# Second layer's experts: half of the tokens gather their experts' rows, the other half multiplies in float32

## The chip, the cores and the metric

The kernel runs on one core of a Trainium2 chip. The metric is the device time of one execution in microseconds, as the median of several runs. A profile of one further execution shows what each engine did in it: PE (TensorE), DVE (VectorE), ACT (ScalarE), POOL (GpSimd) and the queues of transfers, SP's above all.

## What is computed

The program is two blocks of two layers each over 256 tokens of 1024 numbers. The change lies in the first block, in the experts of its second layer. They see the latent tokens alone, two blocks of 128:

```python
def block(hb):                      # 128 tokens at a time
    n = hb.shape[0]
    q = (hb @ w_q).reshape(n, PEER_HEADS, 2, PEER_DK_HALF)      # 8 heads
    s = jnp.einsum('nhpk,pek->nhpe', q, keys)                   # 128 keys for each half
    v_top, i_top = lax.top_k(s, PEER_TOPK)                      # 16
    cand = (v_top[:, :, 0, :, None] + v_top[:, :, 1, None, :]).reshape(n, PEER_HEADS, PEER_TOPK * PEER_TOPK)
    sc, pos = lax.top_k(cand, PEER_TOPK)
    i1 = jnp.take_along_axis(i_top[:, :, 0], pos // PEER_TOPK, axis=-1)
    i2 = jnp.take_along_axis(i_top[:, :, 1], pos % PEER_TOPK, axis=-1)
    e = i1 * N_KEYS + i2                                        # one of 16384 experts
    g = jax.nn.softmax(sc.astype(jnp.float32), axis=-1).astype(hb.dtype)
    a = jax.nn.gelu(jnp.einsum('nhkd,nd->nhk', u_tab[e], hb)) * g
    return jnp.einsum('nhk,nhkd->nd', a, v_tab[e])
```

Each token has 8 x 16 = 128 chosen experts, and an expert is one row of u_tab and one row of v_tab. `x + mod[5] * _peer(h)` is the layer's result.

## The kernel before

A Tile program: the engines' instructions are recorded by helpers and put in order by a scheduler, so an engine's order is not quite that of the code.

There are two ways to the experts' sum. The **dense** way multiplies all tokens with all 16384 rows of U, in 128 blocks of 128 experts (`first`), passes the products through gelu into the tile A, multiplies A by the tokens' weights, zero for experts that were not chosen (`peer_weights`, which builds the weights of 8 tokens at a time from comparisons, f16 products on PE into ps_G and a product on DVE), and multiplies A with the 128 blocks of V (`second`). The **gathered** way fetches for each of the 128 choices the rows of U of 128 tokens by one indirect transfer of POOL (`rows_of`), multiplies them with the tokens on DVE, which sums along the row (line 1409), and later fetches for each token its 128 rows of V and sums them on PE (ps_gv), 32 tokens to a tile.

In the first layer (`peer0`, line 1453) the context tokens go the gathered way beside the dense way of the latent tokens; its first product is float32 (`lin_32`), its second has three parts. In the second layer (`peer`, line 1268, called from line 2323) all 256 latent tokens go the dense way, and both products have three parts: a weight tile is loaded into one of four `raw` buffers by SP's queue, ACT casts it to fp32r (line 350, whi), and DVE or every few times POOL subtracts (line 353, wlo); `hilo` does the same to the activations. `mm3` then makes three matmuls of one. A is a ring of 77 blocks, so the second product starts before the first ends, and a block of U is followed by one of V.

`peer_front` makes the choice: the norm, 16 tiles of queries and their scores, the 16 best of each, the 256 sums of a head, the 16 best of them, and the experts' numbers by comparisons, all on DVE. It yields between its steps, and the caller puts U blocks there. Of `mem_norm`, which prepares the memory tokens for the next block, steps stand in the loops as `side`. The norm of the memory tokens uses the same raw buffers.

Of the kernel before, what the change touches and what calls it, by code (L numbers as in the profile page):

```python
# [188 lines left out]
def prep(I):  # L189
# [18 lines left out]
    for l in range(2):  # L208
# [22 lines left out]
        if l == 0:  # L231
            A["Ur"] = I["peer_u"][l]
# [65 lines left out]
class Kern:  # L298
# [296 lines left out]
    def ctx_ahead(self):  # L595

        while not self.ctx_done:
# [479 lines left out]

    RANGES = {1: (36, 46, 46), 2: (36, 46, 46)}
    RING = {1: 77, 2: 66}
# [4 lines left out]
    def peer_open(self, es, ngroups, ranges=None):  # L1084
# [7 lines left out]
        self.nh = min(ngroups, 2)  # L1092
        self.RG = max(ranges or self.RANGES[ngroups])
# [6 lines left out]
    def peer_front(self, l, s, st, rows=False):  # L1100
# [19 lines left out]
        for j in range(16):  # L1120
            ps = self.psb("ps_q")
            if l == 0:
# [14 lines left out]
        if rows:  # L1137
            self.token_major(h, st)
        else:
            st.update({n: pe.tile([P, NT], FH, tag=n, bufs=self.nh, name=n) for n in ("i1T", "i2T")})  # L1140
            gT = st["gT"] = pe.tile([P, NT // self.TB, 2, self.TB], FH, tag="gT", bufs=self.nh, name="gT")
        for b in range(2):
# [37 lines left out]
            if rows:  # L1180
# [37 lines left out]
    def peer_weights(self, st, A, s0, i0, n):  # L1218
# [5 lines left out]
        def use(t0, pss):  # L1224
            for half in range(NH):
                pv = pss[half][:, :HB * n].rearrange("p (t i) -> p i t", t=HB)
                th = slice(t0 + half * HB, t0 + half * HB + HB)
# [10 lines left out]
        for t0 in range(0, NT, TB):  # L1238
# [13 lines left out]
            if t0:  # L1252
                use(t0 - TB, pss)
# [14 lines left out]
    def peer(self, l, streams, side=()):  # L1268

        nc = self.nc  # L1270
        es = ExitStack()
        self.ctx_done = False
        self.peer_open(es, len(streams))
        pe = self.pe
        self.keys = pe.tile([P, 2, P], FT, name="keys")
        nc.sync.dma_start(self.keys, self.A[f"keys{l}"].rearrange("p (q e) -> p q e", q=2))
        if l:
            self.gains(l, 1)
        sts = [{} for _ in streams]
        fronts = [self.peer_front(l, s, st) for s, st in zip(streams, sts)]  # L1280
        R = self.RING[len(streams)]
        total = P * len(streams)
        A = pe.tile([P, R, NT], FT, name="A")
        pos = {"u": 0, "v": 0}

        def first():
            c = pos["u"]
            pos["u"] += 1
            w = self.weight(self.A[f"U{l}"][c % P])
            ps = self.psb("ps_U")  # L1290
            self.lin_t(w, sts[c // P]["h"], 0, NT, ps)
            nc.scalar.activation(A[:, c % R], ps[:, :NT], AF.Gelu_apprx_tanh)

        acc = None

        def second(c):
            t = A[:, c % R]
            a = (pe.tile([P, NT], FR, tag="a_hi", bufs=2, name="a_hi"),
                 pe.tile([P, NT], FR, tag="a_lo", bufs=2, name="a_lo"))
            self.hilo(a[0], a[1], t)  # L1300
            w = self.weight(self.A[f"V{l}"][c % P])
            for b in range(2):
                bs = slice(b * P, (b + 1) * P)
                for n in range(2):
                    ns = slice(n * 512, (n + 1) * 512)
                    self.mm3(acc[2 * b + n], (a[0][:, bs], a[1][:, bs]), (w[0][:, ns], w[1][:, ns]),
                             c % P == 0, c % P == P - 1)

        def ahead():
            return pos["u"] < total and pos["u"] < pos["v"] + R and sts[pos["u"] // P].get("h") is not None  # L1310


        self.pool_each = 2
        for k, _ in enumerate(fronts[0]):
            self.pool_each = 1 if k in PE1 else 2
            for _ in range(k % 2 if k <= 32 else 2):
                if ahead():
                    first()
        side = fronts[1:] + [f(pe) for f in side]
        ranges = []  # L1320
        for g in range(len(streams)):
            i0 = 0
            for n in self.RANGES[len(streams)]:
                ranges.append((g * P + i0, g, i0, n))
                i0 += n
        gens = [self.peer_weights(sts[g], A, c0 % R, i0, n) for c0, g, i0, n in ranges]
        NB = NT // self.TB + 1
        more = R - pos["u"]
        for k, _ in enumerate(gens[0]):
            for _ in range((k + 1) * more // NB - k * more // NB):  # L1330
                first()
        self.pool_each = 4
        nr, left = 1, NB
        for c in range(total):
            pos["v"] = c
            if c % P == 0:
                acc = [self.psa("ps_acc") for _ in range(4)]
            if nr < len(ranges):
                c0, g, i0, n = ranges[nr]
                if pos["u"] >= c0 + n:  # L1340
                    if left == NB and g and i0 == 0:
                        while "done" not in sts[g]:
                            self.advance(side)
                    k = -(-left // max(1, c0 - c - 1))
                    self.pool_each = 1 if pos["u"] == total else 4
                    for _ in range(min(k, left)):
                        next(gens[nr])
                        left -= 1
                    if left == 0:
                        nr, left = nr + 1, NB  # L1350
            second(c)
            self.pool_each = 4
            pos["v"] = c + 1
            if ahead():
                first()
            self.advance(side)
            if c % P == P - 1:
                self.peer_out(l, streams[c // P], acc)
                self.ctx_done = True
        self.advance(side, 1000)  # L1360
        es.close()

# [3 lines left out]
    def gather_open(self, st):  # L1366

        nc, pe = self.nc, self.pe
        st["ht"] = pe.tile([P, 2, D], FT, name="ht")
        st["g"] = pe.tile([P, 2, P], FT, name="gr")  # L1370
        st["d"] = pe.tile([P, 2, P], FT, name="dots")
        st["e"] = pe.tile([P, 2, P], U32, name="er")
        st["eT"] = pe.tile([P, 2, P], U32, name="eT")
# [6 lines left out]
    def token_major(self, h, st):  # L1380

        nc = self.nc
        for b in range(2):
# [973 lines left out]
```

## Time and profile before

| | us |
|---|---|
| median of 3 runs | 4083.49 |
| lowest, highest | 4080.9, 4084.05 |
| the profiled execution | 4071.07 |
| its span in the trace | 4069.2 |

The trace is one execution, and its stretches are told in us from the span's start. An engine's busy time is the union of its instructions; PEld is the loading of stationary operands, which runs beside PE. A matmul's recorded duration includes time in which the next is already under way, so prices of products are taken from the spacing of their starts. A float32 matmul of the code appears as two instructions. The granted clock is given as a share of 2.4 GHz.

### The profile page before, as it was taken

The page shows a single profiled execution, that of the slowest core. Times are in us where ns is not written, and L with a number is a line of the kernel's source. Part 1 is how long each engine was busy: PE and PEld are TensorE (multiplying, and loading weights), DVE is VectorE, ACT ScalarE, POOL GpSimd, SP SyncE. Part 2 cuts the span into 40 slices and gives each one's busy share as a digit, 9 for nine tenths or more (in the row PEclk, how much of TensorE's full clock was granted, in tenths as well). Part 3 has the DMA queues.
Part 4 walks back from the last instruction along what each step waited for, and adds up shares of the span by engine and source line. Part 5 has one row for each costly group of instructions (what it writes and reads, how often), then busy time and mean ns, then how long its engine had stood idle before and what let it go on. Part 6 is the DMA issues. An engine that isn't in the chain of part 4 may idle for free. (4 is left out here: it accounts for less than half of the span.)

```text
span 4069.2 us, 69007 instructions
## 1 busy us (share of the span) xinstructions
PE 3736.2 (92%) x26811; PEld 3164.7 (78%) x26811; DVE 2718.9 (67%) x5739; ACT 1522.1 (37%) x2552; POOL 1333.6 (33%) x916
## 2 busy tenths in 40 slices
PE   8999996866898889999799988999999999999999
PEld 6777875755676666666589988889778899999999
DVE  5833368788787642374585799886785666864785
ACT  6433320111121211233455443444334646553554
POOL 0022205432435434455314456322442131231122
PEclk9999997987898999999899999999999999999999
DMA  5254238965989889999545544556446413565355
GB/s 211 70 166 140 79 119 281 334 218 192 355 306 365 333 312 354 336 353 403 194 130 163 160 146 126 160 168 191 150 146 189 144 48 113 178 198 179 92 178 151
DMA packets 228952, 827.48 MB, mean 203 GB/s; under 512 B 25736, under 2 KB 27408, under 8 KB 228624
## 3 DMA queue, kind: packets, MB, share of 16 engines
q1 hardware_dynamic: 154752, 554.08, 42.2%
q0 software_dynamic: 73728, 268.47, 17.8%
q8 instruction: 211, 3.46, 0.3%
q14 instruction: 117, 0.96, 0.1%
q10 hardware_dynamic: 144, 0.52, 0.0%
HBM read 821.91 MB, written 1.06 MB: 202 GB/s over the span
## 5 line engine op out<-in xcount | busy, mean ns | idle before, releaser
L350 ACT CAST whi<-raw 128x1024 fp32r<-128x1024 f32 (+1 forms) x774 | 802.0, 1039 | 975.8 <-DMA raw<-in_V 322.0
L353 POOL TENSOR_TENSOR wlo<-raw,whi 128x1024 fp32r<-128x1024 f32 (+1 forms) x230 | 570.6, 2482 | 1457.8 <-ACT whi L350 1308.5
L353 DVE TENSOR_TENSOR wlo<-raw,whi 128x1024 fp32r<-128x1024 f32 (+1 forms) x544 | 670.2, 1233 | 459.8 <-ACT whi L350 454.6
L1394 POOL DMA_INDIRECT gb<-in_Ur,er x256 | 329.6, 1288 | 536.0 <-DVE gb L1409 300.3
L323 PE MATMUL ps_U<-h,raw 128*128 128x256 f32 x2048 | 483.1, 392 | 23.9 <-ACT A L1481 23.7
L323 PEld LDWEIGHTS ps_U<-h,raw 128*128 128x128 f32 x2048 | 398.5, 197 | 93.7 <-ACT A L1481 24.6
L323 PE MATMUL ps_acc<-wlo,a_hi 128*128 128x512 f32 x1024 | 420.6, 411 | 46.2 <-DVE wlo L353 43.7
L323 PE MATMUL ps_acc<-whi,a_hi 128*128 128x512 f32 x1024 | 430.2, 424 | 15.4 <-ACT whi L350 15.4
L323 PE MATMUL ps_acc<-whi,a_lo 128*128 128x512 f32 x1024 | 415.7, 406 | 0.0
L1409 DVE SCALAR_TENSOR_TENSOR gb<-gb,ht 128x1024 f32<-128x1024 f32 x256 | 310.2, 1223 | 124.3 <-DMA gb<-in_Ur,er 123.1
L363 ACT CAST a_hi<-A 128x256 fp32r<-128x256 f32 x256 | 103.5, 405 | 568.4 <-PE ps_acc L323 525.5
L323 PE MATMUL ps_U<-h_hi,whi 128*128 128x256 f32 x1024 | 294.3, 287 | 7.9 <-DVE A L1232 5.4
L323 PE MATMUL ps_U<-h_hi,wlo 128*128 128x256 f32 x1024 | 291.4, 285 | 8.4 <-DVE wlo L353 6.5
L323 PE MATMUL ps_U<-h_lo,whi 128*128 128x256 f32 x1024 | 290.8, 284 | 0.0
L323 PEld LDWEIGHTS ps_acc<-wlo,a_hi 128*128 128x128 f32 x1024 | 200.5, 196 | 95.3 <-DVE wlo L353 53.3
L323 PE MATMUL ps_in<-hh_hi,whi 128*128 128x256 f32 (+1 forms) x776 | 265.9, 345 | 1.7 <-ACT hh_hi L568 1.7
L323 PE MATMUL ps_in<-hh_hi,wlo 128*128 128x256 f32 (+1 forms) x776 | 262.3, 339 | 1.1 <-POOL wlo L353 1.1
L323 PEld LDWEIGHTS ps_acc<-whi,a_hi 128*128 128x128 f32 x1024 | 198.6, 195 | 83.0 <-ACT whi L350 20.7
L323 PE MATMUL ps_in<-hh_lo,whi 128*128 128x256 f32 (+1 forms) x776 | 262.9, 340 | 0.0
L364 DVE TENSOR_TENSOR a_lo<-A,a_hi 128x256 fp32r<-128x256 f32 x256 | 117.5, 460 | 201.8 <-ACT a_hi L363 199.7
L1394 POOL DMA_INDIRECT gb<-in_V,eT x170 | 182.5, 1073 | 178.0 <-PE ps_gv L323 145.4
L323 PEld LDWEIGHTS ps_acc<-whi,a_lo 128*128 128x128 f32 x1024 | 200.6, 196 | 47.6 <-DVE a_lo L364 0.6
(636 smaller groups left out, 8748.9 us busy)
## 6 DMA issues: line engine op xcount, KB each, us to landing
raw<-in_U SPq DMA_DIRECT2D x256, 512.0 KB, 4.3
raw<-in_V SPq DMA_DIRECT2D x256, 512.0 KB, 4.5
raw<-in_win SPq DMA_DIRECT2D x96, 512.0 KB, 3.8
raw<-in_wup SPq DMA_DIRECT2D x88, 512.0 KB, 3.8
raw<-in_wada SPq DMA_DIRECT2D x80, 512.0 KB, 4.8
raw<-in_wq SPq DMA_DIRECT2D x48, 512.0 KB, 4.5
raw<-in_gwin SPq DMA_DIRECT2D x37, 512.0 KB, 3.7
raw<-in_wdn SPq DMA_DIRECT2D x32, 512.0 KB, 4.1
```

The costliest lines, as they stand in the source:

```text
L323: self.nc.tensor.matmul(o, l, r, start=start, stop=stop)
L350: nc.scalar.copy(hi[:, :f], raw[:, :f])
L353: eng.tensor_sub(lo[:, :f], raw[:, :f], hi[:, :f].bitcast(FT))
L363: (copy or self.nc.scalar.copy)(hi, src)
L364: self.nc.vector.tensor_sub(lo, src, hi.bitcast(FT))
L1394: self.nc.gpsimd.indirect_dma_start(t, None, table, bass.IndirectOffsetOnAxis(ap=at, axis=0), bounds_check=P * P - 1, oob_is_err=False)
L1409: nc.vector.scalar_tensor_tensor(t, t, 1.0, st["ht"][:, b], op0=OP.mult, op1=OP.mult, accum_out=st["d"][:, b, j:j + 1])
```

## The change

The host passes U as plain rows for the second layer too (`Ur1`). `peer` with its ring is replaced by `peer1`. The tokens of block 0 go the gathered way, those of block 1 the dense way, in float32 without splits: 8 matmuls of 128 columns to a block of U and 2 of 512 columns to a block of V. A holds all 128 blocks for 128 tokens. The choice is still made for all 256 tokens, now in float32, and ends for block 0 with the experts' numbers (er), their transpose (eT) and the weights (gr) as in the first layer, for block 1 as before. The rows land in six buffers that held the split weights, and after the U rows in the tile of the tokens as a seventh. `peer_weights` gets a first token T0 and works in two ranges of 64 blocks.

```diff
     def peer_front(self, l, s, st, rows=()):
...
-        if l == 0:
-            h = self.hs[s]
-        else:
-            h = tuple(pe.tile([P, KC, NT], FR, name=n) for n in ("h_hi", "h_lo"))
+        h = self.hs[s]
...
-            if l == 0:
-                self.lin_32(self.load_w(self.A["wq0"][j]), h, ps[:, :NT])
-            else:
-                self.lin_t(self.weight(self.A[f"wq{l}"][j]), h, 0, NT, ps)
+            self.lin_32(self.load_w(self.A[f"wq{l}"][j]), h, ps[:, :NT])
...
         if rows:
-            self.token_major(h, st)
-        else:
+            self.token_major(h, st, rows)
+        if len(rows) < 2:
...
-    def gathered(self, st):
+    def gathered(self, st, l, s, nb):
...
-        U, V = self.A["Ur"], self.A["V0"].rearrange("a b d -> (a b) d")
+        U, V = self.A[f"Ur{l}"], self.A[f"V{l}"].rearrange("a b d -> (a b) d")
...
+    RANGES1 = (64, 64)
+
+    def peer1(self, side=()):
...
+        self.gather_open(st, 1)
+
+        st["buf"] += [self.sp.tile([P, D], FT, tag=t, bufs=3, name="gb") for _ in range(3) for t in ("whi", "wlo")]
+        self.hs = (None, pe.tile([P, KC, NT], FT, name="h32"))
+        A = pe.tile([P, P, P], FT, name="A")
...
+        gath = self.gathered(st, 1, 1, 1)
+
+        def units(n):
+            credit[0] += n
+            while credit[0] >= 1 and not self.gathered_all:
+                next(gath)
+                credit[0] -= 1
+
+        def first():
+            c = u[0]
+            u[0] += 1
+            ps = self.psb("ps_U")[:, :P]
+            self.lin_32(self.load_w(self.A["U1"][c]), st["h"][:, :, P:], ps)
+            nc.scalar.activation(A[:, c], ps, AF.Gelu_apprx_tanh)
+
+        for k, _ in enumerate(self.peer_front(1, 1, st, (0,))):
+            first()
+            if "blocks" in st:
+                units(1)
+        side = [f(pe) for f in side]
+        gens = [self.peer_weights(st, A, i0, i0, 64, P) for i0 in (0, 64)]
+        while u[0] < P:
+            first()
+            units(1.5)
+            self.advance(side)
+            if u[0] >= 64:
+                next(gens[0], None)
...
+        acc = [self.psa("ps_acc") for _ in range(2)]
+        for c in range(P):
+            if c >= 4 and c % 3 == 0 or c == 63:
+                for _ in range(1 if c < 63 else P):
+                    next(gens[1], None)
+            w = self.load_w(self.A["V1"][c])
+            for n in range(2):
+                self.mm(acc[n], A[:, c], w[:, n * 512:(n + 1) * 512], c == 0, c == P - 1)
+            units(1.05)
+            self.advance(side)
...
-        self.peer(1, (1,), [lambda pool: self.mem_norm(0, 20)])
+        self.peer1([lambda pool: self.mem_norm(0, 20)])
```

The scheduler turns this into new orders. In the order's rows h_19920 is the normed tokens, raw a weight tile, gb a row buffer, Z_19910 and Z_19911 the tiles that take the gathered tokens' weights, dots the sums of the row products, R and sq the sums of squares of the memory tokens; a line's number is that of the kernel it is from.

**PE, at the end of the front.** Before, the last products of a query tile and the first of a U block:

```order
L323 MATMUL ps_q<-h_hi,whi 128x256
L323 MATMUL ps_q<-h_lo,whi 128x256
L323 MATMUL ps_q<-h_hi,wlo 128x256
L323 MATMUL ps_U<-h_hi,whi 128x256
L323 MATMUL ps_U<-h_lo,whi 128x256
L323 MATMUL ps_U<-h_hi,wlo 128x256
```

Now, from the last scores to the transposes of the experts' numbers (ps_eT for block 0, ps_iT for block 1):

```order
L322 MATMUL ps_U<-h_19920,raw 128x128 x8
L322 MATMUL ps_q<-h_19920,raw 128x256 x8
L322 MATMUL ps_U<-h_19920,raw 128x128 x8
L322 MATMUL ps_s<-keys,qT 128x128 x2
L322 MATMUL ps_U<-h_19920,raw 128x128 x8
L327 MATMUL ps_ht<-cst,h_19920 128x128 x8
L322 MATMUL ps_U<-h_19920,raw 128x128 x48
L327 MATMUL ps_eT<-cst,idx 128x128
L322 MATMUL ps_U<-h_19920,raw 128x128 x56
L327 MATMUL ps_iT<-cst,idx 128x128
```

The three kinds of part products are gone; 33 blocks of U stand ahead of ps_ht and six behind it, ahead of the transpose that the gathered tokens' choice ends with.

**POOL, through the stage.** Before, the low parts of weights (wlo) and the sums of squares of `mem_norm`:

```order
L353 TENSOR_TENSOR wlo<-raw,whi 128x1024
L527 TENSOR_TENSOR R<-R,sq 128x256 x2
L353 TENSOR_TENSOR wlo<-raw,whi 128x1024 x80
L527 TENSOR_TENSOR R<-R,sq 128x256 x7
L353 TENSOR_TENSOR wlo<-raw,whi 128x1024 x59
```

Now, from the clearing of the two Z tiles:

```order
L1271 MEMSET Z_19910 128x512
L1271 MEMSET Z_19911 128x512
L1289 DMA gb<-in_Ur,er 128x1024 x44
L526 TENSOR_TENSOR R<-R,sq 128x256
L1289 DMA gb<-in_Ur,er 128x1024
L526 TENSOR_TENSOR R<-R,sq 128x256 x6
L1289 DMA gb<-in_Ur,er 128x1024 x83
L1289 DMA gb<-in_V,eT 128x1024 x4
```

All 128 gathers of U stand in POOL's order, with the seven sums among them, and those of V follow directly.

**PE, at the turn to the second product.** Before, where a block of V is followed by one of U:

```order
L323 MATMUL ps_acc<-whi,a_lo 128x512
L323 MATMUL ps_acc<-whi,a_hi 128x512
L323 MATMUL ps_acc<-wlo,a_hi 128x512
L323 MATMUL ps_acc<-whi,a_lo 128x512
L323 MATMUL ps_U<-h_hi,whi 128x256
L323 MATMUL ps_U<-h_lo,whi 128x256
L323 MATMUL ps_U<-h_hi,wlo 128x256
```

Now:

```order
L322 MATMUL ps_U<-h_19920,raw 128x128 x390
L322 MATMUL ps_acc<-raw,A 128x512 x24
L327 MATMUL ps_aT<-cst,dots 128x128
L322 MATMUL ps_acc<-raw,A 128x512
L322 MATMUL ps_gv<-gb,Z_19910 32x256 x8
```

U and V no longer alternate: 390 matmuls, the last 48 blocks of U and a part of one, stand in a row, then twelve blocks of V, then the transpose of the row products (ps_aT), and only behind it the first rows of V.

## Rows read from the trace of the kernel before

**Rows 1.** page's first part: busy us (share of span) and instructions

```profile
PE 3736.2 (92%) x26811; PEld 3164.7 (78%) x26811; DVE 2718.9 (67%) x5739; ACT 1522.1 (37%) x2552; POOL 1333.6 (33%) x916
```

**Rows 2.** stretches: length, busy PE PEld DVE ACT POOL (x), PEclk, DMA, GB/s

```profile
2239.00:2346.00 107.00, 102.14 (x843) 100.87 (x842) 83.15 (x327) 52.36 (x90) 42.26 (x17) 0.98 0.53 161
2346.00:2450.00 104.00, 81.10 (x634) 79.61 (x633) 101.70 (x184) 42.11 (x67) 54.82 (x22) 0.92 0.45 142
2450.00:2890.00 440.00, 430.92 (x3672) 392.03 (x3672) 340.07 (x499) 193.01 (x295) 154.44 (x65) 0.99 0.55 165
2890.00:3157.00 267.00, 250.52 (x1498) 195.45 (x1497) 195.68 (x273) 109.97 (x163) 101.33 (x42) 0.99 0.53 158
```

**Rows 3.** groups, same stage: form xcount | busy us, mean ns | idle before

```profile
L323 PE MATMUL ps_U<-h_hi,whi 128*128 128x256 f32 x1024 | 294.3, 287 | 7.9 <-DVE A L1232 5.4 <-ACT whi L350 2.6
L323 PE MATMUL ps_acc<-whi,a_hi 128*128 128x512 f32 x512 | 208.8, 408 | 0.0
L350 ACT CAST whi<-raw 128x1024 fp32r<-128x1024 f32 x273 | 285.7, 1048 | 254.8 <-PE ps_U L323 90.0 <-POOL wlo L353 73.3 <-issue 65.2
L353 POOL TENSOR_TENSOR wlo<-raw,whi 128x1024 fp32r<-128x1024 f32 x137 | 347.9, 2541 | 547.9 <-ACT whi L350 543.3 <-DMA raw<-in_U 3.7 <-POOL wlo L353 0.6
L353 DVE TENSOR_TENSOR wlo<-raw,whi 128x1024 fp32r<-128x1024 f32 x136 | 168.2, 1238 | 60.8 <-ACT whi L350 60.3
```

**Rows 4.** TensorE's timeline, first layer: start us, us, engine, line, form

```profile
1016.63 3.61 PE L323 MATMUL ps_U<-h,raw 128*128 128x256 f32 x16
1020.08 0.38 PE L328 MATMUL ps_adaT<-cst,adar 128*128 128x128 f32 x2
```

**Rows 5.** one tile's products: ns min/median/max, first and last start us

```profile
L323 PE MATMUL ps_c<-bl,raw x128: 273/275/377, 3733.4 to 3749.6; 128*128 128x128 f32 x128
```

**Rows 6.** TensorE's timeline around two gathered rows of the first layer

```profile
1841.36 0.39 PE L323 MATMUL ps_acc<-whi,a_lo 128*128 128x512 f32 x1
1841.67 1.07 PE L323 MATMUL ps_gv<-gb,Z 128*32 128x256 f32 x16
1842.68 0.50 PE L323 MATMUL ps_acc<-whi,a_hi 128*128 128x512 f32 x1
```

**Rows 7.** the weight products' group in the stage of rows 3

```profile
L323 PE MATMUL ps_G<-Pg,P 128*128 128x46 f16 x1024 | 40.7, 185 | 16.5 <-DVE Pg L1250 14.7 <-ACT a_hi L363 0.2
```

**Rows 8.** stretches of the first layer's experts, columns as in rows 2

```profile
1000.00:1380.00 380.00, 322.36 (x1907) 248.12 (x1907) 286.33 (x590) 74.11 (x132) 181.28 (x139) 0.90 0.94 348
1040.00:1060.00 20.00, 16.54 (x59) 12.75 (x60) 13.29 (x22) 3.08 (x5) 10.56 (x8) 0.73 1.00 378
1360.00:1380.00 20.00, 12.84 (x53) 8.81 (x51) 12.10 (x21) 3.17 (x5) 9.94 (x9) 0.74 0.95 363
1560.00:1640.00 80.00, 80.00 (x579) 55.46 (x578) 18.28 (x35) 14.94 (x27) 40.66 (x38) 1.00 0.97 358
1800.00:1940.00 140.00, 139.40 (x1003) 89.42 (x1001) 61.22 (x91) 47.15 (x70) 76.42 (x73) 1.00 1.02 401
1940.00:1960.00 20.00, 13.15 (x122) 2.99 (x122) 0.66 (x2) 0.00 (x0) 14.89 (x15) 0.80 0.99 379
```

**Rows 9.** weight tile's transfer (KB, us to landing), and gathers on POOL

```profile
raw<-in_U SPq DMA_DIRECT2D x256, 512.0 KB, 4.3
L1394 POOL DMA_INDIRECT gb<-in_Ur,er x256: 987/1002/2046, 627.0 to 1372.0; - x128
```

**Rows 10.** VectorE's row products, from the page's fifth part

```profile
L1409 DVE SCALAR_TENSOR_TENSOR gb<-gb,ht 128x1024 f32<-128x1024 f32 x256 | 310.2, 1223 | 124.3 <-DMA gb<-in_Ur,er 123.1
```

**Rows 11.** VectorE's timeline, first half's choice, its first and last step

```profile
2350.03 2.74 DVE L1147 TENSOR_TENSOR cand<-vt 128x512 f32<-128x512 f32 x1
2398.39 0.28 DVE L1204 TENSOR_TENSOR gT<-ps_iT,gT 128x128 f16<-128x128 f32 x1
```

**Rows 12.** timeline, end of the stage: product and last updates of X

```profile
3151.46 0.39 PE L323 MATMUL ps_acc<-whi,a_lo 128*128 128x512 f32 x1
3153.91 3.22 DVE L1571 SCALAR_TENSOR_TENSOR X<-ps_yT,mods,X 128x256 f32<-128x256 f32 x8
```

More of the change, by code (lines that the diff above doesn't have):

```diff
@@ L595, in ctx_ahead @@
     def ctx_ahead(self):
-        while not self.ctx_done:
+        while not self.gathered_all:
             yield
@@ L1137, in peer_front @@
         if rows:
[L1138 to L1141 removed]
+            self.token_major(h, st, rows)
+        if len(rows) < 2:
+            st.update({n: pe.tile([P, NT], FH, tag=n, name=n) for n in ("i1T", "i2T")})
+            gT = st["gT"] = pe.tile([P, NT // self.TB, 2, self.TB], FH, tag="gT", name="gT")
         for b in range(2):
@@ L1237, in peer_weights @@
         H = TB // TQ
-        for t0 in range(0, NT, TB):
+        for t0 in range(T0, NT, TB):
             ts = slice(t0, t0 + TB)
@@ L1266, in peer_weights @@
         yield
[L1268 to L1361, printed above, removed]
@@ L1378, in gather_open, with token_major @@
         st["n"] = 0
-    def token_major(self, h, st):
+    def token_major(self, h, st, blocks):
         nc = self.nc
-        for b in range(2):
+        for b in blocks:
             for n in range(2):
@@ L1419, in gathered @@
             aT.append(a)
-        st["buf"] += [st["ht"][:, b] for b in range(2)]
-        for g in range(NT // 32):
+        st["buf"] += [st["ht"][:, b] for b in range(nb)]
+        for g in range(nb * P // 32):
             po = self.psb("ps_gv")[:, :256]
@@ L1467, in peer0 @@
         credit = [0.0]
-        gath = self.gathered(sc)
+        gath = self.gathered(sc, 0, 0, 2)
+        t = self.in_hh(1, "gb", FT, (P, 4, D))
+        sc["buf"] += [t[:, i] for i in range(4)]
         def units(n=None):
             credit[0] += self.UNITS if n is None else n
-            while credit[0] >= 1 and not self.ctx_done:
+            while credit[0] >= 1 and not self.gathered_all:
                 next(gath)
@@ L1544, in peer0 @@
                 units()
-            if not self.ctx_done:
+            if not self.gathered_all:
                 self.advance(side)
@@ L1552, in peer0 @@
         self.pool_each = 4
+        es.close()
+    RANGES1 = (64, 64)
+    def peer1(self, side=()):
+        nc = self.nc
+        es = ExitStack()
+        self.gathered_all = False
+        self.peer_open(es, self.RANGES1)
+        pe = self.pe
+        self.keys = pe.tile([P, 2, P], FT, name="keys")
+        nc.sync.dma_start(self.keys, self.A["keys1"].rearrange("p (q e) -> p q e", q=2))
+        self.gains(1, 1)
+        st = {}
+        self.gather_open(st, 1)
+        st["buf"] += [self.sp.tile([P, D], FT, tag=t, bufs=3, name="gb") for _ in range(3) for t in ("whi", "wlo")]
+        self.hs = (None, pe.tile([P, KC, NT], FT, name="h32"))
+        A = pe.tile([P, P, P], FT, name="A")
+        u = [0]
+        credit = [0.0]
+        gath = self.gathered(st, 1, 1, 1)
+        def units(n):
+            credit[0] += n
+            while credit[0] >= 1 and not self.gathered_all:
+                next(gath)
[18 more added lines that the diff above has]
+                next(gens[0], None)
+        for _ in gens[0]:
+            units(1)
+        acc = [self.psa("ps_acc") for _ in range(2)]
[8 more added lines that the diff above has]
+            self.advance(side)
+        for n in range(2):
+            y = pe.tile([P, 512], FT, tag="y", bufs=2, name="y")
+            nc.scalar.copy(y, acc[n])
+            ps = self.psb("ps_yT")
+            for k in range(4):
+                self.tr(ps[:, k * P:(k + 1) * P], y[:, k * P:(k + 1) * P])
+            for k in range(4):
+                dc = 4 * n + k
+                xv = self.X[:, dc, P:]
+                nc.vector.scalar_tensor_tensor(xv, ps[:, k * P:(k + 1) * P], self.mods[1][:, 40 + dc, 1:2], xv,
+                                               op0=OP.mult, op1=OP.add)
+        for _ in gath:
+            pass
+        self.advance(side, 1000)
```

53 lines of the change are left out of this document (24 added, 29 removed).

## The prediction

> **What bounds the kernel now.** I read the page's head first, then the stretches of the second layer's experts, then the groups of that stage, and last the rows of the first layer, where the gathered and the float32 forms already run. The head shows a kernel that lives on TensorE: 3736 of 4069 us [rows 1]. The changed stage runs from 2239 us (the mixer's last update of X) to 3157 us (the experts' last one), 918 us [rows 2, 12]. In its four stretches PE is busy 102.1 of 107, 81.1 of 104, 430.9 of 440 and 250.5 of 267 us, together 864.7 us or 94%, at a granted clock of 0.92 to 0.99, while the transfers take about half of the DMA engines: 142 to 165 GB/s [rows 2]. So the stage is bound by products, not by bytes. Rows 3 show where they come from: every expert block has 24 products of 256 columns (three groups of 1024 for 128 blocks, one is shown) and 12 of 512 columns, because each float32 product is made of three of a rounded type; for that, ACT casts each of 273 weight tiles (1048 ns), and DVE or POOL forms each low part (1238 and 2541 ns). What the reader is to see in rows 8 is the other limit: stretches in which the DMA engines are busy 0.94 to 1.02 of the time.
>
> **What the change removes.** For the dense half only 128 of 256 tokens are left, so the products shrink and become plain float32. All 273 splits of this stage go, on three engines at once: ACT 285.7, POOL 347.9 and DVE 168.2 us [rows 3], and so do the casts and low parts of the activations. None of these was waited for long, so I give no gain of their own. The ring goes too: all 128 blocks' results stay in memory.
>
> **What it adds.** 256 gathers of 128 rows, each 512 KB like a weight tile [rows 9], that is 134 MB more for a stage that moved 147 MB (918 us at the GB/s of rows 2); on DVE 128 row products of 1.22 us [rows 10]; on PE the sums of the gathered rows.
>
> **Prices of the float32 products.** One block of 256 columns takes 16 matmul instructions, and 3.45 us pass from its start to the next group's start [rows 4]. For 128 columns the lower end is half, 1.73 us; the upper end is 16 times the spacing of float32 matmuls of 128 columns, (3749.6 - 3733.4)/127 = 0.128 us [rows 5], 2.04 us. I take 1.9. The second matrix has 2 products of 512 columns, 4 instructions of twice 0.216 us: 1.73 us. Two gathered rows cost PE 1.09 us, from 1841.36 plus the 0.23 us of one matmul to 1842.68 [rows 6], so 0.55 each. The weight products (ps_G) cost 40.7 us per 1024 [rows 7]; 32 steps of 16 are 20 us.
>
> **The front.** PE's idle 5 us of the first stretch, around the norm, stay. The program now issues a query tile (3.45 us), its scores (4 matmuls, 0.51 us) and two first-matrix blocks (3.8 us) sixteen times: 125 us, and one block more. That ends at 2239 + 5 + 125 + 2 = 2371 us. Then DVE must finish the experts' numbers of the gathered tokens; PE waits at the transpose of these numbers, and so does the first gather on POOL. Before, the same piece lasted from 2350.03 to 2398.39, 48 us [rows 11], with splits between its instructions and some of them stretched (the first addition took 2.74 us). The ends are 0 and 48; I take 28, because the instructions are the same but the five or so subtractions of 1.24 us and the stretched ones go with POOL's splits. So the gathers begin near 2400 us.
>
> **From the first gather to the end.** Two queues now feed the stage: SP's, with the blocks still to load, and POOL's. By the order of PE, 39 first-matrix blocks are issued ahead of the transpose, so 89 remain, with 128 second-matrix blocks, 4 tiles of the memory tokens, 128 U rows and 128 V rows: 477 transfers of 0.524 MB, 250 MB. PE's work in the same time is 89 x 1.9 + 128 x 1.73 + 128 x 0.55 + 20 = 481 us. The transfers take longer at any rate the trace shows: 624 us at 401 GB/s, 699 at 358, 719 at 348 [rows 8]. I take 380 GB/s: gathers alone reach 379, the mixture of loads and gathers that kept PE full 401, and the first layer's long U stretch, in which PE and the buffers also held the transfers back, 348. That is 658 us. The DMA page bears on this very number. The Trainium skill, page "DMA: Bandwidth & Descriptors", section Specifications, gives a core a limit of about 358 GB/s from memory; by it the stage would end some 40 us later than by my rate, but the 401 GB/s over 140 us of rows 8 lie above it, and the measurement decides.
>
> Beside these transfers lie DVE's row products (128 x 1.22 = 156 us) and its weights, and POOL's issue of gathers at about 1.3 us each [rows 9], 333 of 658 us; these cost nothing as long as six row buffers keep the queue supplied. SP's order has all U ahead of all V, with four buffers, so loads run ahead of the gathers: PE does its last 48 blocks and then twelve V blocks without DVE, and waits at the transpose of the row products until all U rows are in. Behind that wait stand the V products, but the V gathers go on, so the DMA engines are not idle. Late next is the first product that waits for a V row.
>
> After the last transfer come the copies and transposes of the result. Before they ran from the last product near 3151.5 to 3157 us [rows 12], about 6 us; I take 8 with the landing.
>
> **The sum.** 2400 + 658 + 8 = 3066 instead of 3157: 91 us less. The profiled execution took 4071.07 us, so 3980; the median of the three runs lies 12.4 us above that execution, so I forecast **3992 us**. The order outside the stage is the same instruction for instruction but for the handover at its ends, so nothing is added there.
>
> **Rivals.**
> 1. The transfers reach the full 401 GB/s. For it: 140 us of it with both queues filled [rows 8]. Against: a U phase has not shown it. 658 becomes 624 us: 3958 us.
> 2. The transfers hold only 348 to 358 GB/s, the rate of the first layer's long stretches. For it: the 380 us from 1000 to 1380, with the same pair of queues. Against: there PE also had three-part products, and four row buffers fed the gathers, here six. 719 us: 4053 us; within 0.2% of before if the 48 us piece of the front does not shrink either.
> 3. The clock, and slower than before. Products that wait for bytes leave PE idle; in such stretches the clock fell: 0.73 with PE busy 16.5 of 20 us, 0.74 with 12.8 of 20 [rows 8], that is, part of the time at 1.2 instead of 2.4 GHz. Whoever waits then multiplies at half speed, and the queues wait for PE's buffers in turn. The price: 481 us of products at 0.74 are 650; with the 17% idle that stood beside 0.73 it is 783 us instead of 658, the stage ends at 3191, 34 us later than before: 4117 us. It decides from 749 us on (3157 - 8 - 2400), which with 17% idle is a clock under 481/(0.83 x 749) = 0.77. Against it: the stretch at 401 GB/s kept a clock of 1.00, and a lower clock fills the idle time that caused it. The Trainium skill speaks against this change here: "TensorE: Matmul & The Clock Gate", section "HAM oscillation — how this bites in real kernels", tells of a kernel whose products wait for each next transfer and start at the low clock each time. By that rule this rival would be the forecast; the trace agrees for some stretches (0.73) and not for others (1.00).
>
> That the change doesn't do what it says I exclude: the order shows float32 products of 128 columns and 256 gathers in this stage.
>
> **How the numbers follow.** About 0.2% (8 us) is what a measurement of this kernel can tell from no change. The forecast has 0.60, rival 1 has 0.12, rival 2 has 0.18, rival 3 has 0.10. Faster: 0.60 + 0.12 + 0.14 of rival 2 = 0.86; no difference: 0.04 of rival 2 and 0.01 of rival 3, 0.05; slower: 0.09. The range reaches from below rival 1 with the float32 blocks at their lower end in the front (33 blocks of 0.17 us less) and a front piece of 16 us instead of 28 (together 18 us, so 3958 - 18 = 3940) to above rival 2 with a front piece of some 45 us (4070); rival 3 is left out.
>
> **What would show it.** Right: PE busy falls below 80% from about 2400 us on, the transfers there at 360 to 400 GB/s, the stage's end near 3066; the U blocks of 128 columns at 1.7 to 2.0 us; no splits in the stage; POOL only issues gathers. Wrong: a granted clock under 0.8 over the V phase with PE nearly full; a DMA share under 0.85 with gathers waiting for DVE's row products, which would mean that buffers and not bytes set the pace; or a first gather much later than 2400 us.

## The result, and the profile after

The median fell from 4082.19 us (4 runs, 4077.23 to 4084.05) to **3961.06 us** (4 runs, 3959.37 to 3966.28): ratio 0.9707, 95% interval 0.969 to 0.9724, 121 us less where the prediction had 91. The profiled execution took 3959.87 us. The page's first part, which answers to [rows 1]:

```profile
PE 3552.3 (90%) x24642; PEld 2838.3 (72%) x24642; DVE 2345.2 (59%) x5406; ACT 1201.6 (30%) x2156; POOL 1253.4 (32%) x1037
```

A stage is counted here from the start of the mixer's last update of X to the start of the experts' last one: 2239.3 to 3156.7 us before, 917.4 us, and 2246.0 to 3050.1 us now. (The last one is the dense tokens' in all kernels but filled_front and filled_and_paced, where the gathered tokens' comes later.) It falls into three parts: the **front** up to the transpose of the experts' numbers (ps_eT), behind which the gathers begin; the **U phase** up to the transpose of the row products (ps_aT); and the **V phase**. The stretches of the changed kernel, with the columns of [rows 2]; the last row is the whole stage:

```profile
2246.00:2401.90 155.90, 137.77 (x959) 129.67 (x957) 83.64 (x405) 31.90 (x86) 1.11 (x2) 0.94 0.58 187
2401.90:2728.90 327.00, 228.37 (x1734) 199.34 (x1735) 225.89 (x435) 39.99 (x118) 155.71 (x139) 0.91 0.98 378
2728.90:3050.10 321.20, 314.12 (x1779) 111.98 (x1780) 43.98 (x111) 6.83 (x13) 123.27 (x125) 0.99 1.01 397
2246.00:3050.10 804.10, 680.26 (x4471) 440.99 (x4470) 353.51 (x950) 78.72 (x217) 280.10 (x265) 0.95 0.91 349
```

The stage is 113.3 us shorter. The transfers went from about half of the engines to all of them, 0.98 and 1.01. TensorE is busy 70% of the U phase, but 98% of the V phase, which the prediction had not foreseen. From the groups (idle before, and what ended it), 2200 to 3100 us:

```profile
L1303 DVE SCALAR_TENSOR_TENSOR gb<-gb,ht 128x1024 f32<-128x1024 f32 x128 | 156.7, 1230 | 99.8 <-DMA gb<-in_Ur,er 99.6
L1289 POOL DMA_INDIRECT gb<-in_Ur,er x128 | 142.8, 1116 | 320.0 <-DVE er L1173 155.4 <-DVE gb L1303 140.5 <-DVE eq L1159 6.8
L1289 POOL DMA_INDIRECT gb<-in_V,eT x110 | 110.2, 1002 | 147.5 <-PE ps_gv L322 139.9 <-DVE gb L1303 4.3 <-issue 1.5
```

POOL issues a gather as soon as a row buffer is given back, by DVE in the U phase (140.5 us of waiting), by TensorE in the V phase (139.9). These waits alone don't say which is the bound, since a buffer also comes back late when its row lands late; that is what the experiments are for.

The first gather, from the timeline. Behind the six U blocks of the first line TensorE has waited 14.43 us for the experts' numbers; the gather follows at 2402.52, where the prediction had 2400:

```profile
2376.44 11.00 PE L322 MATMUL ps_U<-h,raw 128*128 128x128 f32 x96
2401.86 0.45 PE L327 MATMUL ps_eT<-cst,idx 128*128 128x128 f32 x1 [14.43 <-DVE idx L1172]
...
2402.52 1.22 POOL L1289 DMA_INDIRECT gb<-in_Ur,er  x1 [155.41 <-DVE er L1173]
```

Two stretches of the U phase, columns as above. In the second they move 409 GB/s at a share of 1.03, though TensorE is idle a fifth of the time; in the first DVE is full and the share falls to 0.72:

```profile
2520.00:2530.00 10.00, 4.96 (x52) 4.65 (x53) 10.00 (x23) 1.68 (x5) 2.83 (x2) 0.83 0.72 265
...
2630.00:2640.00 10.00, 7.86 (x65) 7.20 (x64) 4.93 (x8) 1.11 (x4) 3.72 (x4) 1.00 1.03 409
```

### The profile page after: what moved, and what is told of

The parts are those of the page before. It is cut to its first block, busy times and chain, and to the rows that moved or that the text cites. A ratio compares the mean times of both kernels' runs of the same rounds, so it can differ in the third digit from the quotient of the medians.

```text
span 3958.1 us, 63943 instructions
## 1 busy us (share of the span) xinstructions
PE 3552.3 (90%) x24642; PEld 2838.3 (72%) x24642; DVE 2345.2 (59%) x5406; ACT 1201.6 (30%) x2156; POOL 1253.4 (32%) x1037
## 5 line engine op out<-in xcount | busy, mean ns | idle before, releaser
L322 PE MATMUL ps_U<-h,raw 128*128 128x256 f32 (+1 forms) x4096 | 758.0, 342 | 63.8 <-DMA raw<-in_U 37.5
L322 PEld LDWEIGHTS ps_U<-h,raw 128*128 128x128 f32 x4096 | 657.7, 201 | 145.4 <-ACT A L1485 36.1
L349 ACT CAST whi<-raw 128x1024 fp32r<-128x1024 f32 (+1 forms) x502 | 517.7, 1034 | 751.0 <-DMA raw<-in_V 340.4
L352 POOL TENSOR_TENSOR wlo<-raw,whi 128x1024 fp32r<-128x1024 f32 (+1 forms) x93 | 222.0, 2387 | 929.0 <-ACT whi L349 733.0
L322 PE MATMUL ps_acc<-raw,A 128*128 128x512 f32 x512 | 256.1, 621 | 8.0 <-DMA raw<-in_V 7.8
L322 PE MATMUL ps_acc<-wlo,a_hi 128*128 128x512 f32 x512 | 216.7, 423 | 45.3 <-DVE wlo L352 45.1
L322 PE MATMUL ps_acc<-whi,a_hi 128*128 128x512 f32 x512 | 220.0, 437 | 12.4 <-ACT whi L349 12.4
L322 PE MATMUL ps_acc<-whi,a_lo 128*128 128x512 f32 x512 | 211.9, 414 | 0.0
L322 PE MATMUL ps_gv<-gb,Z 128*32 128x256 f32 x2240 | 172.5, 398 | 9.6 <-DMA gb<-in_V,eT 8.9
L322 PE MATMUL ps_q<-h,raw 128*128 128x256 f32 x768 | 176.3, 382 | 0.0
```

Of the source, the lines that this page charges most:

```text
L322: self.nc.tensor.matmul(o, l, r, start=start, stop=stop)
L349: nc.scalar.copy(hi[:, :f], raw[:, :f])
L352: eng.tensor_sub(lo[:, :f], raw[:, :f], hi[:, :f].bitcast(FT))
```

## Experiments

The theory: from the first gather on the bytes set the pace, at a ceiling near 409 GB/s, and TensorE only fills. The rivals: TensorE sets the pace of the V phase, where it is busy 98%; DVE or the number of row buffers sets that of the U phase. "V ahead" is the number of V blocks that stand ahead of ps_aT in TensorE's order; they count to the U phase, with their loads. Beside these groups of experiments the kernel before had medians between 4078.48 and 4086.95 us, so a few us between two medians of the table say nothing. The argument goes by the stages, each of which is read from one trace.

| kernel | median us | front us | U phase us (GB/s) | V phase us (GB/s) | stage us | V ahead |
|---|---|---|---|---|---|---|
| changed | 3961.06 | 155.9 | 327.0 (378) | 321.2 (397) | 804.1 | 12 |
| changed_again | 3964.0 | 154.7 | 330.8 (374) | 320.2 (398) | 805.7 | 12 |
| half_v_products | 3972.17 | 154.6 | 331.8 (377) | 321.5 (397) | 807.9 | 14 |
| half_u_rows | 3920.0 | 154.6 | 264.6 (321) | 337.6 (395) | 756.8 | 0 |
| four_row_buffers | 3981.87 | 155.8 | 340.4 (365) | 323.3 (392) | 819.5 | 14 |
| six_gathers | 3875.61 | 155.8 | 225.4 (226) | 329.3 (209) | 710.5 | 0 |
| late_sums_and_weights | 3956.78 | 155.8 | 294.0 (396) | 339.7 (396) | 789.5 | 3 |
| filled_front | 3954.03 | 154.6 | 333.7 (377) | 304.2 (402) | 792.5 | 22 |
| choice_in_halves | 3948.24 | 74.2 | 365.1 (381) | 353.4 (384) | 792.7 | 0 |
| filled_and_paced | 3942.43 | 155.8 | 315.5 (393) | 315.7 (394) | 787.0 | 22 |
| halves_balanced | 3965.95 | 74.6 | 410.0 (369) | 314.2 (393) | 798.8 | 21 |
| halves_sums_later | 3960.38 | 74.6 | 411.2 (374) | 303.7 (398) | 789.5 | 25 |

**half_v_products**

```diff
             w = self.load_w(self.A["V1"][c])
-            for n in range(2):
+            for n in range(1):
                 self.mm(acc[n], A[:, c], w[:, n * 512:(n + 1) * 512], c == 0, c == P - 1)
```

> This run leaves out the products of the second 512 columns of every V block for the dense tokens (128 x 2 of 256 products of 512 columns; the copy of the first half stands in for the second). All loads, gathers, row products and sums stay. It takes 128 x 0.86 = 110 us of work from TensorE, nearly all in the V phase, where TensorE is busy 306 of 312 us. Theory (the bytes set the pace, 399 to 409 GB/s in that phase): the freed time turns into waits for V tiles and rows, the time stays within 12 us of 3961, 3949 to 3961 us, and the DMA share stays at 1.0. Rival (TensorE sets the pace of the V phase): the phase shrinks by most of the 110 us, to about 3865 us.

Measured: a V phase of 321.5 us, against 321.2 with all products. TensorE's work went from 314 to 226 us and nothing came of it:

```profile
2743.60:3065.10 321.50, 226.49 (x1578) 74.03 (x1578) 45.45 (x112) 8.46 (x15) 126.60 (x126) 0.97 1.00 397
```

In its timeline each V block now waits for its tile, and a step of a block and a row takes 2.55 us, two transfers of 0.524 MB at 409 GB/s (2.56):

```profile
2904.45 1.13 PE L322 MATMUL ps_acc<-raw,A 128*128 128x512 f32 x2 [0.66 <-DMA raw<-in_V]
2905.50 0.64 PE L322 MATMUL ps_gv<-gb,Z 128*32 128x256 f32 x8
2907.00 1.12 PE L322 MATMUL ps_acc<-raw,A 128*128 128x512 f32 x2 [0.85 <-DMA raw<-in_V]
2908.05 0.64 PE L322 MATMUL ps_gv<-gb,Z 128*32 128x256 f32 x8
```

So the bytes alone hold the V phase at this length. The median of 3972 lies above the 3961 of the changed kernel, and above the expected 3949 to 3961; in the trace the stage began 11 us later and took 3.8 us more; so the stages, each from its own start, are what is compared.

**half_u_rows**

```diff
         st["n"] += 1
+        if table is self.A["Ur1"] and st["n"] > 6 and st["n"] % 4 in (0, 3):
+            return t
```

> This run leaves out 62 of the 128 gathers of U rows (the row products of those choices take what the buffer holds). DVE's row products, all loads and all matmuls stay. 62 x 0.524 = 32.5 MB less. Theory (bytes at about 409 GB/s): 79 us less, 3882 us. Rival 1 (DVE and the row buffers set the pace of the U phase: DVE is busy 225 of its 328 us and POOL waits 145 us for it): under 25 us less, 3936 us or more. Rival 2 (TensorE): no change.

Measured: 41 us less in the median, 47 in the stage, between the theory (79) and rival 1 (under 25). The U phase lost 62.4 us, more than rival 1 allows, so bytes held it; but not all of that is won. No V block stands ahead of ps_aT in this order, so twelve V blocks with their 6.3 MB went over to the V phase, which took 16.4 us more; there TensorE is full. And the U phase ended at a new bound: DVE is busy 218.7 of 264.6 us and the rate only 321 GB/s:

```profile
2409.60:2674.20 264.60, 196.51 (x1687) 186.89 (x1688) 218.66 (x427) 39.33 (x118) 109.93 (x77) 0.90 0.86 321
2674.20:3011.80 337.60, 333.80 (x1824) 119.80 (x1825) 47.36 (x121) 6.38 (x13) 123.11 (x124) 0.99 1.01 395
```

**four_row_buffers**

```diff
-... for _ in range(3) for t in ("whi", "wlo")]
+... for _ in range(2) for t in ("whi", "wlo")]
```

> Four row buffers instead of six, nothing else. The prediction named the six buffers as the reason why the rate would pass the 348 GB/s of the first layer's long U stretch. A gather lands about 8 us after its issue, and with issue and row product a buffer is taken some 10 us. Theory (the DMA engines' own ceiling sets the pace, and the loads fill what the gathers leave): at most 15 us more, 3961 to 3976 us. Rival (buffers set the rate): the U phase falls to about 348 GB/s, 328 x 379 / 348 = 357 us, and the V phase likewise to some 340: 3961 + 29 + 28, about 4018 us.

Measured: the stage 15.4 us longer, 13.4 of it in the U phase, whose rate is 365 GB/s and not 348; the V phase 2.1 us. That is the theory's upper end (15 us), far from the rival's 57: six buffers are worth some 15 us here, and with four the stage still passes the first layer's 348 GB/s. The expectation had a gather landing about 8 us after its issue; the U rows of the changed kernel's stage take 13.0 us in the median. The median lies 21 us higher, but its four runs spread from 3968.71 to 3993.29.

**six_gathers**

```diff
         st["n"] += 1
+        if st.get("few") and st["n"] > 6:
+            return t
```

> This run leaves out all gathers of this stage but the first six of U rows; row products (their factor 1.0 is now 0.0), sums on TensorE, loads and every order stay. So it shows what the stage costs without the gathers' 131 MB. Theory (bytes): from the first gather on only TensorE's work is left, 481 us by the prediction's prices instead of 640: about 150 to 160 us less, 3800 to 3811 us, with TensorE above 95% in both phases. Rival (TensorE sets the V phase, bytes only the U phase): the U phase falls from 328 to 229 us, the V phase stays: about 3862 us.

Measured: 85 us less in the median, 93.6 in the stage. The theory's 150 fell, and the rival came within 14 us: it had 229 us for the U phase, the V phase unchanged and 3862 us in all. Without the rows both phases stay long, at half of the transfers' rate:

```profile
2410.10:2635.50 225.40, 188.10 (x1686) 184.26 (x1687) 218.53 (x435) 39.84 (x117) 13.70 (x13) 0.91 0.66 226
2635.50:2964.80 329.30, 328.56 (x1828) 119.58 (x1827) 44.25 (x111) 6.82 (x13) 0.00 (x0) 1.00 0.61 209
```

In the U phase DVE is busy 218.5 of 225.4 us: row products, weights and the dense half's choice are the next bound, 102 us below the bytes. In the V phase TensorE is full, for 128 V blocks, since none stands ahead of ps_aT here. Its timeline has a step of 2.48 us:

```profile
2702.12 1.98 PE L322 MATMUL ps_acc<-raw,A 128*128 128x512 f32 x4
2704.03 0.64 PE L322 MATMUL ps_gv<-gb,Z 128*32 128x256 f32 x8
2704.60 1.98 PE L322 MATMUL ps_acc<-raw,A 128*128 128x512 f32 x4
...
2707.09 0.65 PE L322 MATMUL ps_G<-Pg,P 128*128 128x64 f16 x16
2707.58 1.96 PE L322 MATMUL ps_acc<-raw,A 128*128 128x512 f32 x4
```

128 x 2.48 = 317, and 16 groups of weight products at 0.49 us (2707.58 - 2707.09) are 8: 325 of the 329 us. A V block alone takes 0.43 x 4 = 1.72 us, as 24 products in a row show in the changed kernel (10.47 us less the 0.59 of one record, over 23 spacings):

```profile
3034.93 10.47 PE L322 MATMUL ps_acc<-raw,A 128*128 128x512 f32 x24
```

so a row between two blocks costs 2.48 - 1.72 = 0.76 us and not the 0.55 of [rows 6], where two rows stood together. With 116 blocks left the changed kernel's V phase needs, by these prices, 116 x 1.72 + 128 x 0.76 + 8 + 5 for the end = 310 us of TensorE, and its 127.5 MB (321.2 us at 397 GB/s) need 312 us at 409 GB/s. **Worked out so, both limits are the same there, to within a per cent or so**, and taking either away alone frees next to nothing: the run without half of the products found the bytes behind TensorE, this one TensorE behind the bytes (in an order with twelve V blocks more in the phase).

**float32_all_tokens** is the kernel before with `lin_32` for queries and U blocks, `self.mm` on A and the raw tile for V, and no splits:

> One part of the change alone, made to the kernel before: all 256 tokens stay dense, with the ring, but all products of this stage are plain float32 without splits; nothing is gathered. Theory (float32 alone loses, and pays only because half of the tokens leave the dense way): a U block of 256 columns 3.45 us, a V block 8 instructions of 0.43 us, 3.45 us too, 16 query tiles 3.45 us: 128 x 6.9 + 55 + 8 + 41 for the weights = 987 us of TensorE instead of 865, with little idle (10 to 20 us instead of 53): the stage takes about 1000 us instead of 918, so 4165 us, at least 4140. Rival (the splits were the brake of the stage before, and taking them away is what gained): not slower than before, 4085 us or less.

Measured: 4158.41 us, ratio 1.0194 (1.0162 to 1.0225), 80 us slower than before; the stage from 2246.4 to 3250.7, 1004 us, and TensorE full:

```profile
2450.00:2900.00 450.00, 450.00 (x2636) 331.21 (x2635) 131.33 (x370) 43.23 (x105) 5.10 (x7) 1.00 0.43 147
```

The theory had 4165 us and a stage of 1000. So plain float32 without splits, taken together, loses 87 us of stage (1004 - 917); what the splits alone had cost was not measured apart. Sending half of the tokens to the gathers, with the order that goes with it, gives 200 (1004 - 804).

**late_sums_and_weights**

```diff
             units(1.5)
-            self.advance(side)
-            if u[0] >= 64:
+            if u[0] >= 64 and u[0] % 3 == 0:
                 next(gens[0], None)
```

> The changed kernel with two pieces of DVE's work thinned out in the U phase: the norm of the memory tokens advances only beside the V blocks, and the first half of the dense tokens' weights is built at every third U block instead of every one. In the U phase the DMA share fell to 0.72 to 0.95 from 2500 to 2550 us, where DVE was full. Theory (these dips are DVE's, the rest is the ceiling): the dips go, some 8 us less in the U phase, and 0 to 3 us of the norm's sums come back on the full TensorE of the V phase: the stage takes 795 to 800 us instead of 804. Rival 1 (the buffers wait for something else): the U phase stays at 327 us. Rival 2 (more comes back in the V phase): the stage takes 804 us or more.

Measured: the U phase runs at 396 GB/s in 294.0 us, 33 us less, the V phase takes 339.7 us, 18.5 more, and the stage 14.6 less. The dips were DVE's, as one stretch of both traces shows, the changed kernel first:

```profile
2520.00:2540.00 20.00, 11.83 (x96) 10.97 (x96) 19.14 (x44) 3.63 (x11) 6.65 (x5) 0.74 0.77 276
...
2520.00:2540.00 20.00, 14.41 (x111) 13.44 (x110) 15.21 (x28) 1.66 (x6) 8.80 (x9) 0.83 1.03 408
```

But only 3 V blocks stand ahead of ps_aT now. The U phase moves 7 MB less for that (396 GB/s over 294.0 us against 378 over 327.0), some 18 of its 33 us, and they come back in the V phase, where TensorE is busy 332 of 340 us. Net the dips were worth 14.6 us, more than the 4 to 9 that the theory had for the stage.

**filled_front**

```diff
-            first()
+            for _ in range(2 if 32 < k < 40 else 1):
+                first()
```

> The changed kernel with seven more U blocks ahead of the transpose of the gathered tokens' numbers, where TensorE waited 14.4 us and the DMA engines were busy 0.45 of the time; nothing is added or left out. Theory (bytes after the first gather set the pace): seven transfers of 1.28 us leave the later stretch, 9 us less, the stage takes about 795 us instead of 804. Rival (the end is set by TensorE's steps of 2.48 us in the V phase, and by what DVE does in the U phase): 0 to 3 us less.

Measured: the stage 792.5 us, 11.6 shorter, near the theory's 9 and outside the rival's 0 to 3. The U phase took 6.7 us more and the V phase 17.0 less, because the scheduler put 22 V blocks ahead of ps_aT. Here the gathered tokens end last (3044.9 us, the dense ones 3042.4).

**choice_in_halves** (the loop over queries and scores becomes a function of the half; `peer1` issues no U block in the first half's loop; beside the lines shown, `units(1.25)` takes the place of `units(1.5)`, the norm no longer advances beside the U blocks, and the weights come at every fourth of them):

```diff
         for b in range(2):
+            if l:
+                yield from scores(b, 1)
...
-            first()
+            for _ in range(0 if k < 33 else 2 if k < 40 else 1):
+                first()
```

> A try at a better version: queries, scores and choice are done for the gathered half first, without U blocks between, and for the dense half afterwards, beside the gathers; the query weights are loaded twice (16 x 0.524 = 8.4 MB more). The memory tokens' norm moves beside the V blocks, the weights come at every fourth U block. Theory: the first gather comes some 85 us earlier (5 + 16 x 2.15 + 28 = 68 us after the stage's start instead of 156); the U phase then moves 264 transfers, 138 MB, at 378 to 409 GB/s in 338 to 366 us, and the V phase takes 128 steps of 2.48 us and 8 us for the weights, 325 us, with 8 us of tail: the stage takes 740 to 770 us instead of 804, the time is 3897 to 3927 us. Rival (DVE, with the second half's choice beside the row products, becomes the bound of the U phase): the U phase takes over 400 us and the stage 800 us or more.

Measured: the front took 74.2 instead of 155.9 us, the U phase 365 as expected, the V phase 353.4 instead of 325: the stage 792.7, 3948.24 us. Of 82 us won in front 11 are left. Most of the loss is bytes. The changed kernel's front moves 29.2 MB (155.9 us at 187 GB/s), this one 13.8 (74.2 us at 186), and 8.4 MB are loaded twice; so 274.5 MB stand behind the transpose and not 251, which at 387 GB/s are 61 of the 70 us that came back. The theory had counted these transfers; what it had too short is the V phase. No V block stands ahead of ps_aT, and TensorE, idle for 92 us of the U phase, is busy 97% of the time behind it:

```profile
2320.70:2685.80 365.10, 272.63 (x2358) 256.95 (x2357) 243.43 (x577) 41.73 (x152) 150.00 (x135) 0.94 0.98 381
2685.80:3039.20 353.40, 341.52 (x1877) 127.50 (x1875) 53.02 (x130) 15.66 (x37) 126.08 (x128) 0.98 0.99 384
```

**changed_again**

> The changed kernel once more, beside the two tries on the same chip. The stage's start lay between 2239 and 2258 us in the traces so far, in code that no kernel here touches. Expected: 3955 to 3972 us, and a stage of 802 to 808 us from its own start, 321 to 335 us of it from the transpose of the row products on.

Measured: 3964.0 us and a stage of 805.7 us, as expected, with a V phase of 320.2, just under the 321 expected. The two traces of this kernel differ by 1.6 us in the stage and by 3.8 in the U phase.

**filled_and_paced** has the edits of filled_front and late_sums_and_weights, and `units(1.25)` and `units(1.2)` for 1.5 and 1.05.

> The filled front, the late sums and weights, and other paces: 1.25 row units to a U block instead of 1.5, 1.2 instead of 1.05 to a V block, so that 22 V blocks stand ahead of the transpose of the row products instead of 12. Theory (TensorE and the transfers both need nearly the whole stage, 680 us of work each at 409 GB/s, and what counts is that neither waits for the other): V blocks, which take TensorE 1.9 us for 1.28 us of transfer, beside U rows, which take it nothing, keep both busy: the U phase of the filled front at 396 instead of 377 GB/s, 333.7 x 377 / 396 = 318 us, the rest as there: a stage of 774 us. Rival (the single gains of 14 us came from one and the same slack): 787 to 792 us.

Measured: 3942.43 us (3936.0 to 3949.38), ratio 0.9665 (0.9637 to 0.9693), beside 3964.0, 0.9718 (0.9694 to 0.9742), for the changed kernel in the same group. It is the lowest median here of a kernel with nothing left out, but choice_in_halves (0.9678, 0.9649 to 0.9707) can't be told from it. The dense tokens' updates end at 3022.5 us, and the gathered ones' last:

```profile
L1520 DVE SCALAR_TENSOR_TENSOR X<-ps_yT,mods,X x8: 340/340/350, 3020.7 to 3022.5; 128x128 f32<-128x128 f32 x8
L1338 DVE TENSOR_TENSOR X<-X,rg x8: 281/284/285, 2801.6 to 3026.5; 128x128 f32<-128x128 f32 x8
```

So the stage took 787.0 us, 17 to 19 less than in the two traces of the changed kernel. That is the rival's lower edge (787), not the theory's 774: of the single gains, 14.6 and 11.6 us, only a part adds up. The U phase came as expected (315.5 us for 318), the V phase took 315.7 and not the 302 that the theory had for it.

**halves_balanced** is choice_in_halves with `units(0.85)` and `units(1.25)`.

> The choice in halves with 0.85 row units to a U block and 1.25 to a V block, so that 21 V blocks stand ahead of the transpose of the row products instead of none. In the choice in halves TensorE was full in the last 353 us (384 GB/s) and idle 92 of the 365 us before (381 GB/s). Theory (balance): 275 MB at 400 GB/s after a front of 74 us, and 5 us of tail: a stage of about 766 us. Rival (that version was held by something else, DVE in the U phase): 785 to 793 us again.

Measured: 798.8 us. The V phase shrank to 314.2 us, but the U phase took 410 and lost it again. The theory failed, and the trace has a hole: from 2660 to 2740 us no gather was issued. The wait of POOL there, which looked like the cause:

```profile
POOL R L526 <- ACT sqa L549: 87.4, 1, 87.4
```

**halves_sums_later** is halves_balanced with `mem_norm(0, 70)` for `mem_norm(0, 20)` and two U blocks, not one, in six more steps.

> The balanced choice in halves with two edits: the norm of the memory tokens begins 70 steps after the first V block instead of 20, so that its seven sums on POOL stand behind 64 gathers of V rows instead of ahead of all of them, and six more U blocks stand ahead of the transposes of the dense half's choice. In the balanced version POOL waited 87 us at the first of these sums, for the memory tokens' tile, which comes behind V tiles in SP's queue; from 2660 to 2740 us no row was fetched and the DMA share was 0.79 to 0.83; and TensorE waited 25 us at the transposes. Theory (it was this wait of POOL): the share returns to about 1.0, 80 us at 1.03 instead of 0.82 are 16 us less, and 3 to 6 us come from the filled wait: a stage of 777 to 780 us instead of 799. Rival (the gathers waited there for TensorE's or DVE's buffers anyway): 790 us or more.

Measured: 789.5 us, the rival's value. The hole stayed as it was, with another wait in its place:

```profile
POOL gb L1296 <- PE ps_gv L322: 97.6, 7, 90.9
```

A stretch of it, columns as above:

```profile
2700.00:2720.00 20.00, 20.00 (x107) 9.66 (x105) 8.50 (x18) 0.00 (x0) 0.00 (x0) 1.00 0.85 283
```

POOL had filled all seven row buffers with V rows by 2648 us, and their products stand behind ps_aT, behind 25 V blocks, while TensorE was full. In halves_balanced seven V rows were out by 2650 us too, so its gathers would have stopped there without the sums. In this version 25 blocks ahead of that transpose (789.5 us) gain little over none (792.7). Where it would have to stand was not tried, and the number of blocks is not shown to decide by itself: filled_and_paced has 22 and the shortest stage of all that leave nothing out.

## Why the prediction was right, and where its size was off

- **Right: the bound passes from products to bytes.** The DMA share is 0.98 and 1.01 after the first gather, and half_v_products shows that products can go without gain. But the sign that the prediction had named for itself, TensorE busy below 80% from 2400 us on, did not come: it was busy 542.5 of 648.2 us, 84%.
- **Right: the front.** 2371 + 28 = 2399 was the sum; the transpose behind the choice ran at 2401.86, and the stage had begun 7 us later than before, so the front is 5 us shorter than forecast. The 28 us in it was a choice between 0 and 48. The U blocks cost 11.00 us for six, 1.8 us each (forecast 1.9). The stage's own products have no splits left (two casts at its very end, from 3044.9 us on, are for the memory keys of the next block), and POOL issues gathers and, as listed ahead, seven sums.
- **The term that was mis-sized: 658 us at 380 GB/s.** From ps_eT to the last update passed 648.2 us against a forecast of 666 with the tail. The bytes were right: 378 GB/s for 327.0 us and 397 for 321.2 are 251 MB (forecast 250). The rate was 387 GB/s over both phases; what I had taken, 380, was that of gathers alone [rows 8], and it was that of the U phase, while the V phase ran at 397. Those 18 us and 5 of the front make the stage 23 us shorter than forecast: 804 instead of 827 (3066 - 2239). Since it began 7 us later, its end came 16 us early: 3050 instead of 3066.
- **The rest of the 31 us** (3992 - 3961). Behind the stage the way to the end is 4 us shorter (912.1 before, 907.6 now; nothing tried there). The 12.4 us that I added from the profiled execution to the median were before's alone: the changed kernel's profiled execution lies 1.2 us under its median, 11 us less. So 16 + 4 + 11 = 31.
- **Wrong in the size of TensorE's work.** I had 481 us for it beside 658 of transfers, never the limit; it was busy 542.5. A row between two blocks costs 0.76 us instead of 0.55, which is 27 us for 128; the other 34 were not taken apart. And the work is unevenly spread: 70% busy in the U phase, 98% in the V phase. That the time still came out near a forecast from bytes alone is luck: in that phase both limits coincide, and with products a little dearer TensorE would have set it.
- **Rival 1** (401 GB/s, 3958 us) is nearest to the time, though not by its reason: the transfers did not run at 401, they averaged 387. **Rival 2** is out, and with it its reason: with four row buffers the U phase still ran at 365 GB/s. The limit of about 358 GB/s in the Trainium skill, "DMA: Bandwidth & Descriptors", Specifications, stands there as half of a memory stack's 716 GB/s, for one of two cores. The program here runs on one core, and that limit did not bind it: 397 over 321 us.
- **Rival 3**, the clock, decided nothing. The granted clock was 0.91 in the U phase, where TensorE waits, and 0.99 in the V phase, so the prediction's sign of being wrong (under 0.8 there) did not come. half_v_products has 88 us less work in the V phase, waits for a tile at every block, and a clock of 0.97. The slow restart at every transfer that the Trainium skill tells of ("TensorE: Matmul & The Clock Gate", section "HAM oscillation — how this bites in real kernels") is not seen with these gaps of 0.7 to 0.9 us.

## What to carry to other kernels

When work is moved from products to transfers, add up both for each phase, not for the stage: here TensorE's 228 us stood beside 302 us of transfers at 409 GB/s in the U phase, and 310 beside 312 in the V phase, where neither could be cut alone. Price an operation between the neighbours that it will have (a row between two blocks, not two rows). An earlier start of the transfers is worth only what they were idle before it: of 82 us won in front 61 went to bytes that the front had moved and to weights loaded twice. In a static order ask what is held up behind each instruction that waits: seven buffers full of rows, whose products stood behind one transpose, stopped the gathers for 90 us.

## What had not been expected of the hardware

Plain loads and gathers together hold 409 GB/s for a long time, at a share of 1.03 and with TensorE 99% busy. The row is one of five such stretches of 50 us that follow each other in the V phase, from 2750 to 3000 us:

```profile
2850.00:2900.00 50.00, 49.49 (x260) 17.33 (x257) 2.10 (x8) 0.37 (x1) 19.59 (x20) 1.00 1.03 409
```

And the start of the stage varied from 2239 to 2257 us between the traces, in code that none of these kernels touches; the 12.4 us between the profiled execution of before and its median are of that size.
